# Gating one-hots of a PEER layer interleaved over two tokens instead of four, and the late low splits taken off GpSimd

## The chip, the cores and the metric

The kernel runs on one core of a Trainium2 chip. The metric is device time in microseconds from the start to the end of one execution; the median of three runs is given for the kernel before. The profile is of one more execution.

## The reference, cut to what matters

Two transformer blocks on 256 tokens of 1024 features. The part that matters here is the PEER feed-forward, which runs once in each of the first two layers:

```python
def peer_ffn(h, w_query, sub_keys, expert_u, expert_v):
    ...
    scores = jnp.einsum('thpd,hpkd->thpk', q, sub_keys.astype(jnp.float32))
    s_top, i_top = lax.top_k(scores, K)
    cand = (s_top[:, :, 0, :, None] + s_top[:, :, 1, None, :]).reshape(T, Hh, K * K)
    cand_idx = (i_top[:, :, 0, :, None] * PEER_NKEYS + i_top[:, :, 1, None, :]).reshape(T, Hh, K * K)
    best, pos = lax.top_k(cand, K)
    expert_idx = jnp.take_along_axis(cand_idx, pos, axis=-1)
    gates = jax.nn.softmax(best, axis=-1).astype(h.dtype)
    ...
        u = expert_u[idx]
        a = jax.nn.gelu(jnp.einsum('tkd,td->tk', u, xb)) * g
        return jnp.einsum('tk,tkd->td', a, expert_v[idx])
```

Each token picks 128 of 16384 = 128 x 128 experts (8 heads of 16) and sums their outputs with gates.

## The kernel before, in words

The kernel computes all 16384 experts for all tokens and multiplies by a dense gate matrix that is zero where a token did not pick the expert.

**Units.** Weights come as units of 128 x 1024 float32, 512 KB each. `plan` writes out their order by hand; for a weight unit its last field says whether GpSimd (POOL) or VectorE (DVE) makes the low half. `pump` loads units ahead (four raw buffers, queue SP, L274), then splits each into a high part (ScalarE copy, L286) and a low part (subtraction on DVE or POOL, L288) of type fp32r; three split buffers let it run three units ahead. A product is three matmuls (`mm3`, L321 to L323): high x high, high x low, low x high. In `peer` a layer has 128 units `pu` (scores of 128 experts each) and 128 units `pv` (their outputs).

**Which units go to POOL.** Of a layer's `pu` units, those below 64 with i % 4 = 3 (16 of them) and those from 64 on with i % 3 = 2 (65, 68, ... 125: 21 of them) have their low part made on POOL. All `pv` units have it made on DVE.

**PEER stage by stage.** The first 64 `pu` units fill `S1` (experts 0 to 8191) while routing (top-k) runs on DVE beside them. The second 64 fill `S2`, and beside them runs `gating`: per batch of `GT` = 4 tokens one step, 64 steps a layer, put into the queue of tasks from which `tick` takes about one per unit (four units take one more in their middle). Then come the `pv` units, the products with `V`.

**A gating step** has three parts, each of another batch: `scale(b-2)`, `place(b-1)`, `build(b)`.
- `build` (L1141 to L1150): four DVE operations on 128 x 512 fp16. Two compare `iota_rep` with the indices `i1` and `i2` of four tokens, which gives one-hots `o1` and `og[:, 1]`; two multiply the second one-hot by the high and low part of the gate (`g3`). The layout is [expert key, token], the token innermost: each token's column has a step of four fp16 elements, 8 bytes.
- `place` (L1152 to L1158): for each of the four tokens two matmuls of 128 x 128 fp16, `o1` of the token as the stationary operand and `og` of the token as the moving one, summed in PSUM. Eight matmuls a step, 1024 in the kernel.
- `scale` (L1160 to L1168): DVE multiplies the `S1` slice by the gates from PSUM (L1162), ScalarE copies the other half (L1166), and every fourth step POOL stores it to HBM (L1168) for `gate_late`.

On each engine the order is the order of the program: in one unit DVE has the low split of a unit two ahead, then scale, then the four builds; TensorE has 24 matmuls of the unit, then the eight of `place`. `o1` and `og` have two buffers each.

Of the kernel before, what the change touches and what calls it, by code (L numbers as in the profile page):

```python
# [13 lines left out]
F16 = mybir.dt.float16  # L14
# [3 lines left out]
ALU = mybir.AluOpType  # L18
# [4 lines left out]
P = 128  # L23
# [6 lines left out]
GT = 4  # L30
# [123 lines left out]
class Net:  # L154
# [41 lines left out]
    def plan(self):  # L196
        a = self.a
        self.units = u = []

        def ws(src, tag, every=0):  # L200
            return [("w", src[i], tag, bool(every) and i % every == every - 1) for i in range(src.shape[0])]

        def on_pool(units, *which):
            return [(w[0], w[1], w[2], i in which) for i, w in enumerate(units)]

        def cols(l, lo, hi):
            return [("ada", (l, o)) for o in range(lo, hi)]

        def mix(units, jobs=(), per=1, skip=0):
            jobs = deque(jobs)  # L210
            for i, w in enumerate(units):
                u.append(w)
                for _ in range(per if i >= skip else 0):
                    if jobs:
                        u.append(jobs.popleft())
            u.extend(jobs)

        def spread(units, jobs, every, skip):
            jobs = deque(jobs)
            for i, w in enumerate(units):  # L220
                u.append(w)
                if i >= skip and i % every == 1 and jobs:
                    u.append(jobs.popleft())
            assert not jobs

        mk = ws(a["mem_k"], "mem_k")
        mix(on_pool(ws(a["mem_v"], "mem_v"), 2, 4, 6), cols(0, 0, 16), 2)
        mix(on_pool(ws(a["ret_qk"], "ret_qk"), 0, 1, 3))
        mix(ws(a["ret_g"], "ret_g") + ws(a["ret_v"], "ret_v"), cols(0, 16, 40))
        mix(ws(a["ret_o"], "ret_o"))  # L230
        mix(mk[:3])
        for l in range(2):
            pq = ws(a["pq"][16 * l:16 * l + 16], "pq")
            mix(on_pool(pq, 0, 1, 2, 4, 7, 10, 13))
            us = [("w", a["pu"][P * l + i], "pu", i % 4 == 3 if i < 64 else i % 3 == 2)
                  for i in range(P)]
            vs = [("w", a["pv"][P * l + i], "pv", False) for i in range(P)]
            mix(us)
            if l == 0:
                jobs = cols(0, 40, 48) + cols(1, 0, 37)  # L240
                spread(vs[:64], jobs[:17], 3, 13)
                spread(vs[64:], jobs[17:], 2, 9)
            else:
                mix(vs)
            if l == 0:
                mix(on_pool(mk[3:6], 2))
                mix(on_pool(ws(a["sgu_v"], "sgu_v"), 0, 1, 2) + on_pool(ws(a["sgu_u"], "sgu_u"), *range(0, 24, 4)), cols(1, 37, 48), 1, 6)
                mix(ws(a["sgu_o"], "sgu_o", 4))
                mix(mk[6:8])
        for tag in ("hy_v", "hy_qk", "hy_c", "hy_oc", "hy_oa", "mem_q", "mem_o"):  # L250
            mix(ws(a[tag], tag))
        mix(ws(a["mlp_u"], "mlp_u") + ws(a["mlp_d"], "mlp_d"))
        self.n_load = self.n_split = self.w_done = self.w_split = 0
        self.raw = {}
        self.ring = deque()
        self.flying = [0, 0]
        self.split = deque()
# [270 lines left out]
    def run(self):  # L528
        nc, a = self.nc, self.a
        self.plan()  # L530
        c = self.p_c = self.keep("pc")
        self.p_h = self.keep("ph", bufs=4)
        self.p_raw = self.keep("praw", bufs=RAW_BUFS)
        self.p_split = self.keep("psplit", bufs=SPLIT_BUFS)
        self.p_ps = self.keep("pps", bufs=2, space=PSUM)
        self.p_d = self.keep("pd", space=DRAM)
        self.ident = c.tile([P, P], F32, name="ident")
        self.iota = c.tile([P, TOPK], F32, name="iota")
        self.vecs = c.tile([P, _off], F32, name="vecs")
        self.ones = c.tile([P, P], F32, name="ones")  # L540
        self.eps = c.tile([P, 1], F32, name="eps")
        self.iota_rep = c.tile([P, P, GT], F16, name="iota_rep")
        self.mod = [c.tile([P, 48], F32, name=f"mod{l}") for l in range(2)]
        self.d_c = self.p_d.tile([1, D], F32, name="d_c")
        self.d_mk = self.p_d.tile([P, KC, T], F32, name="d_mk")
        self.d_mv = self.p_d.tile([P, 2, D], F32, name="d_mv")
        self.d_mr = self.p_d.tile([P, T], F32, name="d_mr")
        self.d_g = [self.p_d.tile([T // GS, P, 64, GS], F32, name=f"d_g{l}") for l in range(2)]
        self.d_x = [self.p_d.tile([P, KC, T], F32, name=f"d_x{l}") for l in range(2)]
        self.open_x()  # L550
        cm_f, pf = self.pool("pf0")
        cm_s, ps = self.pool("start", side="right")
        cm_e, self.p_early = self.pool("early", bufs=EARLY_BUFS, side="right")
        mem = ps.tile([P, KC, T], F32, name="mem")
        nc.scalar.dma_start(self.vecs, a["vecs"])
        for k in range(2):
            nc.sync.dma_start(mem[:, 4 * k:4 * k + 4], a["memT"][:, 4 * k:4 * k + 4])
        cr = ps.tile([P, D], F32, name="craw")
        nc.scalar.dma_start(cr, a["c"].to_broadcast([P, D]))
        nc.scalar.dma_start(self.x, a["xT"])  # L560
        nc.vector.memset(self.ones, 1.0 / D)
        nc.vector.memset(self.eps, EPS)
        self.const(self.ident, "ident")
        iota = ps.tile([P, P], F32, name="iota_all")
        self.const(iota, "iota")
        self.cs = pf.tile([P, 2, T], F32, name="cs")
        rope = self.rope(ps, self.cs)

        self.mem_n = 0
        self.mem_pend = deque()  # L570
        mh = self.new_h(pf)
        for n in range(KC):
            self.split_scaled([mh[n]], [mem[:, n]], [self.vec("g_mem", n, 1)])
        self.pump(1)
        self.cact = self.p_n.tile([P, D], F32, tag="cact", name="cact")
        nc.scalar.activation(self.cact, cr, AF.Silu)
        nc.gpsimd.dma_start(self.d_c, self.cact[0:1, :])
        self.ms_begin(KC)
        nc.vector.tensor_copy(self.iota, iota[:, :TOPK])
        nc.vector.tensor_copy(self.iota_rep, iota[:, :, None].to_broadcast([P, P, GT]))  # L580
        def squares(src, n):
            return lambda: [self.ms_add(src[:, n + k]) for k in range(4)]
        st = {}

        def total():
            st[0] = self.ms_root(self.ms_sum(), KC)
            self.ms_begin(KC)

        def rstd():
            self.rstd = self.ms_recip(st[0], "rstd")  # L590
        self.pipe([squares(self.x, 0), lambda: (rope[0](), squares(self.x, 4)()), rope[1],
                   lambda: (rope[2](), total(), squares(mem, 0)()), rstd, squares(mem, 4)])
        self.mem_store_v = self.mem_values(mh)
        self.shut(cm_e)
        self.shut(cm_s)
        self.retention(self.rstd)
        self.fill_pool, self.fill_h = cm_f, mh
        self.peer(0)
        self.sgu()
        self.peer(1)  # L600
        self.hybrid()
        self.memattn()
        self.mlp()
        self.shut(self.cm_deep)
        self.shut(self.cm_x)
# [531 lines left out]
    def gating(self, po, S, i1, i2, g3, d_g):  # L1137
        nc = self.nc
        made, mult, stage = {}, {}, {}

        def build(b):  # L1141
            tt = slice(b * GT, b * GT + GT)
            sh = [P, P, GT]
            o1 = po.tile(sh, F16, tag="o1", name="o1")
            og = po.tile([P, 2, P, GT], F16, tag="og", name="og")
            nc.vector.tensor_tensor(o1, self.iota_rep, i1[:, None, tt].to_broadcast(sh), op=ALU.is_equal)
            nc.vector.tensor_tensor(og[:, 1], self.iota_rep, i2[:, None, tt].to_broadcast(sh), op=ALU.is_equal)
            for k in range(2):
                nc.vector.tensor_tensor(og[:, k], og[:, 1], g3[:, k, None, tt].to_broadcast(sh), op=ALU.mult)  # L1149
            made[b] = (o1, og)  # L1150

        def place(b):  # L1152
            o1, og = made.pop(b)
            g = mult[b] = self.st_tile("g").rearrange("p (t c) -> p t c", t=GT)
            for t in range(GT):
                for k in range(2):
                    nc.tensor.matmul(g[:, t], o1[:, :, t], og[:, k, :, t], start=k == 0, stop=k == 1)  # L1157

        def scale(b):
            g = mult.pop(b).rearrange("p t c -> p c t")  # L1160
# [629 lines left out]
```

## Time and profile before

| | us |
|---|---|
| median of 3 runs | 2640.93 (2640.41 to 2640.95) |
| the profiled execution | 2635.87 |
| its span, first to last instruction | 2634.1 |
| TensorE (PE) busy | 2552.9 (97%) |
| weight loads (PEld) busy | 2488.4 (94%) |
| VectorE (DVE) busy | 1937.0 (74%) |
| ScalarE (ACT) busy | 1262.2 (48%) |
| GpSimd (POOL) busy | 405.5 (15%) |

The share of busy time is an average over stages. Matmuls overlap in their records, so the length of one record is longer than the distance from one to the next; the distance is what a matmul costs in a stream. The chain that ended last is followed back from the last instruction to whatever released each step.

### The profile page before, as it was taken

The page shows a single profiled execution, that of the slowest core. Times are in us where ns is not written, and L with a number is a line of the kernel's source. Part 1 is how long each engine was busy: PE and PEld are TensorE (multiplying, and loading weights), DVE is VectorE, ACT ScalarE, POOL GpSimd, SP SyncE. Part 2 cuts the span into 40 slices and gives each one's busy share as a digit, 9 for nine tenths or more (in the row PEclk, how much of TensorE's full clock was granted, in tenths as well). Part 3 has the DMA queues.
Part 4 walks back from the last instruction along what each step waited for, and adds up shares of the span by engine and source line. Part 5 has one row for each costly group of instructions (what it writes and reads, how often), then busy time and mean ns, then how long its engine had stood idle before and what let it go on. Part 6 is the DMA issues. An engine that isn't in the chain of part 4 may idle for free.

```text
span 2634.1 us, 49904 instructions
## 1 busy us (share of the span) xinstructions
PE 2552.9 (97%) x20358; PEld 2488.4 (94%) x20358; DVE 1937.0 (74%) x3148; ACT 1262.2 (48%) x1790; POOL 405.5 (15%) x252
## 2 busy tenths in 40 slices
PE   5999999999999999999999999999999999989998
PEld 3989999999999999988999999999999999879998
DVE  8777688889868767775777888888675555785754
ACT  4445444444444445455554444444444444665643
POOL 5000312222221000020132222222100000101001
PEclk9999999999999999999999999999999999999999
DMA  7685555554559788867564555555675655444553
GB/s 285 225 301 168 191 176 185 179 174 161 182 177 336 254 299 273 274 229 239 168 208 166 180 181 180 175 166 176 211 278 184 216 185 184 156 136 149 174 189 116
DMA packets 146406, 532.34 MB, mean 202 GB/s; under 512 B 16080, under 2 KB 18256, under 8 KB 145280
## 3 DMA queue, kind: packets, MB, share of 16 engines
q1 hardware_dynamic: 133104, 481.36, 54.9%
q0 software_dynamic: 11584, 45.56, 4.7%
q8 instruction: 160, 2.62, 0.4%
q10 hardware_dynamic: 1488, 2.23, 0.2%
q14 instruction: 70, 0.57, 0.1%
HBM read 506.93 MB, written 22.16 MB: 201 GB/s over the span
## 4 chain that ended last, share of the span: by engine, by line
PE 81%; DVE 9%; DMA 5%; ACT 3%; issue 2%; POOL 0%; DVEq 0%; ACTq 0%; SPq 0%; POOLq 0%
PE pu L322 11%; PE pu L321 11%; PE pu L323 11%; PE V L322 8%; PE V L323 8%; PE V L321 8%; PE g L1157 4%; PE po L322 3%; PE po L323 3%; PE po L321 3%; DVE split L288 2%; ACT split L286 2%; DMA raw<-in_pv 1%; PE pq L322 1%; PE pq L323 1%
## 5 line engine op out<-in xcount | busy, mean ns | idle before, releaser
L288 DVE TENSOR_TENSOR split<-raw,split 128x1024 fp32r<-128x1024 f32 x698 | 856.7, 1231 | 559.9 <-ACT split L286 559.0
L286 ACT ACTIVATE split<-raw 128x1024 fp32r<-128x1024 f32 x808 | 851.4, 1057 | 728.5 <-PE V L323 328.8
L321 PE MATMUL pu<-h,split 128*128 128x256 f32 x2496 | 718.8, 288 | 0.1
L322 PE MATMUL pu<-h,split 128*128 128x256 f32 x2496 | 706.8, 283 | 0.5 <-DVE h L381 0.5
L323 PE MATMUL pu<-h,split 128*128 128x256 f32 x2496 | 705.5, 283 | 1.1 <-POOL split L288 0.9
L323 PE MATMUL V<-a_sp,split 128*128 128x256 f32 x2048 | 579.4, 283 | 2.3 <-DVE split L288 2.3
L322 PE MATMUL V<-a_sp,split 128*128 128x256 f32 x2048 | 579.3, 283 | 0.1
L321 PE MATMUL V<-a_sp,split 128*128 128x256 f32 x2048 | 579.1, 283 | 0.2 <-ACT split L286 0.2
L321 PEld LDWEIGHTS pu<-h,split 128*128 128x128 f32 x2496 | 479.4, 192 | 0.8 <-ACT u L1323 0.3
L322 PEld LDWEIGHTS pu<-h,split 128*128 128x128 f32 x2496 | 477.9, 191 | 1.3 <-DVE h L381 0.7
L323 PEld LDWEIGHTS pu<-h,split 128*128 128x128 f32 x2496 | 477.2, 191 | 1.7 <-POOL split L288 1.3
L288 POOL TENSOR_TENSOR split<-raw,split 128x1024 fp32r<-128x1024 f32 x110 | 276.4, 2513 | 782.9 <-ACT split L286 780.7
L323 PEld LDWEIGHTS V<-a_sp,split 128*128 128x128 f32 x2048 | 392.3, 192 | 3.1 <-DVE split L288 3.1
L322 PEld LDWEIGHTS V<-a_sp,split 128*128 128x128 f32 x2048 | 392.2, 192 | 0.5 <-DVE a_sp L375 0.5
L321 PEld LDWEIGHTS V<-a_sp,split 128*128 128x128 f32 x2048 | 392.3, 192 | 0.4 <-ACT split L286 0.4
L879 ACT ACTIVATE S<-pu 128x512 f32<-128x512 f32 x128 | 76.6, 598 | 273.1 <-PE pu L323 273.1
L1149 DVE TENSOR_TENSOR og<-og,g 128x512 f16<-128x512 f16 x256 | 150.4, 588 | 8.8
L1157 PE MATMUL g<-og,o 128*128 128x128 f16 x1024 | 143.3, 295 | 1.4 <-DVE og L1149 1.4
L408 POOL TENSOR_TENSOR ms_acc<-ms_acc,sq 128x256 f32<-128x256 f32 x45 | 51.4, 1142 | 569.6 <-ACT sq L406 566.1
L293 DVE SCALAR_TENSOR_TENSOR raw<-raw,cact 128x1024 f32<-128x1024 f32 x96 | 126.9, 1329 | 3.2 <-issue 1.6
L1157 PEld LDWEIGHTS <-o 128*128 128x128 f16 x1024 | 103.9, 118 | 9.8 <-issue 2.5
L322 PE MATMUL pq<-h,split 128*128 128x256 f32 x320 | 93.3, 292 | 5.7 <-DVE h L468 4.0
(370 smaller groups left out, 4049.9 us busy)
## 6 DMA issues: line engine op xcount, KB each, us to landing
raw<-in_pu SPq DMA_DIRECT2D x256, 512.0 KB, 3.3
raw<-in_pv SPq DMA_DIRECT2D x256, 512.0 KB, 4.1
raw<-in_ada SPq DMA_DIRECT2D x96, 512.0 KB, 4.7
raw<-in_pq SPq DMA_DIRECT2D x32, 512.0 KB, 4.1
d_g<-stage POOLq DMA_DIRECT2D x32, 512.0 KB, 3.7
g<-d_g POOLq DMA_DIRECT2D x16, 1024.0 KB, 8.6
raw<-in_mlp_u SPq DMA_DIRECT2D x32, 512.0 KB, 3.4
raw<-in_mlp_d SPq DMA_DIRECT2D x32, 512.0 KB, 3.3
```

The costliest lines, as they stand in the source:

```text
L286: nc.scalar.activation(s[:, 0], r, AF.Copy)
L288: eng.tensor_sub(s[:, 1], r, s[:, 0].bitcast(F32))
L293: nc.vector.scalar_tensor_tensor(r, r, 1.0, self.cact, op0=ALU.mult, op1=ALU.mult, accum_out=self.mod[l][:, o:o + 1])
L321: mm(ps, w_hi, x_hi, start=start, stop=False, **kw)
L322: mm(ps, w_hi, x_lo, start=False, stop=False, **kw)
L323: mm(ps, w_lo, x_hi, start=False, stop=stop, **kw)
L408: nc.gpsimd.tensor_add(self.ms_parts[0], self.ms_parts[0], sq)
L879: nc.scalar.activation(S[:, i - 1:i + 1], pt, AF.Gelu_apprx_tanh)
L1149: nc.vector.tensor_tensor(og[:, k], og[:, 1], g3[:, k, None, tt].to_broadcast(sh), op=ALU.mult)
L1157: nc.tensor.matmul(g[:, t], o1[:, :, t], og[:, k, :, t], start=k == 0, stop=k == 1)
```

## The change

Per batch of four tokens the one-hots have the layout [pair of tokens, expert key, token of the pair] instead of [expert key, token]: a token's column has a step of two fp16 elements, 4 bytes, instead of four, 8 bytes. `iota_rep` shrinks from 128 x 4 to 128 x 2 and is read twice by a broadcast. The four DVE operations of `build` keep their 512 elements; their innermost runs have two elements. The eight matmuls of `place` read the same values from the other places. Second, of the `pu` units from 64 on none has its low part made on POOL: these 21 a layer (42 in all) go to DVE.

```diff
-            us = [("w", a["pu"][P * l + i], "pu", i % 4 == 3 if i < 64 else i % 3 == 2)
-                  for i in range(P)]
+            us = [("w", a["pu"][P * l + i], "pu", i < 64 and i % 4 == 3) for i in range(P)]
...
-        self.iota_rep = c.tile([P, P, GT], F16, name="iota_rep")
+        self.iota_rep = c.tile([P, P, 2], F16, name="iota_rep")
...
-        nc.vector.tensor_copy(self.iota_rep, iota[:, :, None].to_broadcast([P, P, GT]))
+        nc.vector.tensor_copy(self.iota_rep, iota[:, :, None].to_broadcast([P, P, 2]))
...
         def build(b):
             tt = slice(b * GT, b * GT + GT)
-            sh = [P, P, GT]
+            sh = [P, GT // 2, P, 2]
+
+            def pairs(v):
+                return v.rearrange("p (a c) -> p a c", c=2)[:, :, None, :].to_broadcast(sh)
+
             o1 = po.tile(sh, F16, tag="o1", name="o1")
-            og = po.tile([P, 2, P, GT], F16, tag="og", name="og")
-            nc.vector.tensor_tensor(o1, self.iota_rep, i1[:, None, tt].to_broadcast(sh), op=ALU.is_equal)
-            nc.vector.tensor_tensor(og[:, 1], self.iota_rep, i2[:, None, tt].to_broadcast(sh), op=ALU.is_equal)
+            og = po.tile([P, 2] + sh[1:], F16, tag="og", name="og")
+            io = self.iota_rep[:, None].to_broadcast(sh)
+            nc.vector.tensor_tensor(o1, io, pairs(i1[:, tt]), op=ALU.is_equal)
+            nc.vector.tensor_tensor(og[:, 1], io, pairs(i2[:, tt]), op=ALU.is_equal)
             for k in range(2):
-                nc.vector.tensor_tensor(og[:, k], og[:, 1], g3[:, k, None, tt].to_broadcast(sh), op=ALU.mult)
+                nc.vector.tensor_tensor(og[:, k], og[:, 1], pairs(g3[:, k, tt]), op=ALU.mult)
             made[b] = (o1, og)
...
-                    nc.tensor.matmul(g[:, t], o1[:, :, t], og[:, k, :, t], start=k == 0, stop=k == 1)
+                    nc.tensor.matmul(g[:, t], o1[:, t // 2, :, t % 2], og[:, k, t // 2, :, t % 2],
+                                     start=k == 0, stop=k == 1)
```

## Rows read from the trace of the kernel before

**Rows 1.** The page: engines' busy time, and the last chain by engine.
```profile
PE 2552.9 (97%) x20358; PEld 2488.4 (94%) x20358; DVE 1937.0 (74%) x3148; ACT 1262.2 (48%) x1790; POOL 405.5 (15%) x252
...
PE 81%; DVE 9%; DMA 5%; ACT 3%; issue 2%; POOL 0%; DVEq 0%; ACTq 0%; SPq 0%; POOLq 0%
```
**Rows 2.** Windows of both gating stretches: length, busy PE, PEld, DVE, ACT, POOL; PEclk, DMA, GB/s.
```profile
530.00:774.00 244.00, 243.32 (x2031) 239.01 (x2030) 209.63 (x361) 102.68 (x160) 56.87 (x36) 1.00 0.51 173
1636.00:1880.00 244.00, 243.25 (x2029) 238.70 (x2027) 209.72 (x362) 102.83 (x161) 56.87 (x36) 1.00 0.52 173
```
**Rows 3.** Timeline of PE around one step: start us, length us, instruction, count.
```profile
547.01 0.28 PE L322 MATMUL pu<-h,split 128*128 128x256 f32 x1
547.13 0.28 PE L323 MATMUL pu<-h,split 128*128 128x256 f32 x1
547.26 1.11 PE L1157 MATMUL g<-og,o 128*128 128x128 f16 x8
...
548.33 0.28 PE L322 MATMUL pu<-h,split 128*128 128x256 f32 x1
```
**Rows 4.** Groups by line and form, PE: busy us, mean ns of one, idle before.
```profile
L322 PE MATMUL pu<-h,split 128*128 128x256 f32 x2496 | 706.8, 283 | 0.5 <-DVE h L381 0.5
...
L1157 PE MATMUL g<-og,o 128*128 128x128 f16 x1024 | 143.3, 295 | 1.4 <-DVE og L1149 1.4
...
L355 PE MATMUL pv<-split,h 128*128 128x512 f32 x176 | 70.5, 401 | 5.2 <-DVE split L288 3.3 <-POOL split L288 1.9
```
**Rows 5.** Timeline of PE in a stream of 512-column matmuls.
```profile
167.83 0.40 PE L355 MATMUL pv<-split,h 128*128 128x512 f32 x1
168.06 0.39 PE L356 MATMUL pv<-split,h 128*128 128x512 f32 x1
```
**Rows 6.** Groups by line and form, weight loads.
```profile
L322 PEld LDWEIGHTS pu<-h,split 128*128 128x128 f32 x2496 | 477.9, 191 | 1.3 <-DVE h L381 0.7
...
L1157 PEld LDWEIGHTS <-o 128*128 128x128 f16 x1024 | 103.9, 118 | 9.8 <-issue 2.5
...
L1487 PEld LDWEIGHTS po<-pT,v 128*64 128x64 f32 x16 | 1.4, 137 | 0.3
```
**Rows 7.** Lines 1146 and 1149 (build): durations ns least/median/most, first and last start.
```profile
L1146 DVE TENSOR_TENSOR o<-iota_rep,i x128: 416/419/2473, 524.9 to 1863.0; 128x512 f16<-128x512 f16 x128
...
L1149 DVE TENSOR_TENSOR og<-og,g x256: 424/425/2517, 525.7 to 1864.3; 128x512 f16<-128x512 f16 x128
```
**Rows 8.** Groups of DVE, 524 to 775 us.
```profile
L1149 DVE TENSOR_TENSOR og<-og,g 128x512 f16<-128x512 f16 x128 | 75.2, 588 | 4.4
L288 DVE TENSOR_TENSOR split<-raw,split 128x1024 fp32r<-128x1024 f32 x45 | 55.1, 1224 | 29.5 <-ACT split L286 29.5
L1146 DVE TENSOR_TENSOR o<-iota_rep,i 128x512 f16<-128x512 f16 x64 | 45.1, 705 | 0.0
```
**Rows 9.** Groups of POOL, 524 to 775 us.
```profile
L288 POOL TENSOR_TENSOR split<-raw,split 128x1024 fp32r<-128x1024 f32 x21 | 50.5, 2407 | 114.5 <-ACT split L286 114.5
```
**Rows 10.** Timeline of POOL and DVE around one POOL split.
```profile
548.66 2.40 POOL L288 TENSOR_TENSOR split<-raw,split 128x1024 fp32r<-128x1024 f32 x1 [3.31 <-ACT split L286]
...
548.87 2.47 DVE L1146 TENSOR_TENSOR o<-iota_rep,i 128x512 f16<-128x512 f16 x1
```
**Rows 11.** Waits of PE, 530 to 774 us (total, times, longest); PE's timeline at one.
```profile
PE g L1157 <- DVE og L1149: 0.7, 4, 0.2
...
539.08 0.28 PE L323 MATMUL pu<-h,split 128*128 128x256 f32 x1
...
539.74 0.98 PE L1157 MATMUL g<-og,o 128*128 128x128 f16 x7 [0.17 <-DVE og L1149]
...
540.67 0.28 PE L322 MATMUL pu<-h,split 128*128 128x256 f32 x1
```
**Rows 12.** Groups by form, DVE: two operations of 512 elements elsewhere.
```profile
L375 DVE TENSOR_TENSOR a_sp<-S,a_sp 128x512 fp32r<-128x512 f32 x128 | 87.5, 685 | 0.9 <-ACT a_sp L374 0.9
...
L1091 DVE TENSOR_TENSOR tree<-tree 128x512 bf16<-128x512 bf16 x8 | 3.4, 427 | 0.3
```

## Prediction

> **What bounds the kernel now.** I read the page's busy times and last chain first: TensorE is busy 97% of the span and makes up 81% of the chain [rows 1]. The average settles nothing for one stage, so next come the windows of the two stretches in which gating runs, 244 us each. There PE is busy 243.3 us of 244 at the full granted clock, 1.00, which is the 2.4 GHz level; DVE is busy 209.6, ACT 102.7, POOL 56.9, DMA half [rows 2]. So these stretches are PE streams without holes, with DVE 34 us behind, and what the eight matmuls of a step cost on PE is paid in full. PE's waits say the same from the other side: 0.7 us in the first stretch, four times, for the builds [rows 11].
>
> Then the timeline of one step. The distance between two `pu` matmuls is 0.12 us. From the last of them before the step to the second one after it pass 548.33 - 547.13 = 1.20 us [rows 3]; less two ordinary distances that is 0.96 us for eight gating matmuls, 0.12 us each. A matmul with 128 columns thus takes as long as a `pu` matmul with 256. Over 1024 of them this is 123 us of the kernel.
>
> **Part one, the step of the operands.** Nothing is added on PE: the same 1024 matmuls and weight loads with a 4-byte step in place of 8. What is a column worth at either step? A 256-column `pu` matmul lasts 283 ns and a 512-column one 401 [rows 4]: 118 ns for 256 columns, 0.46 ns a column, with some 165 ns that do not depend on them. These read 4-byte elements one behind the other, a 4-byte step. The gating matmul lasts 295 ns with 128 columns; less the same 165 that is 130 ns, 1.02 ns a column, a little over twice as much. At 0.46 ns its columns would take 59 and the record would last about 224. The nearest row to the changed access is therefore the `pu` row: other type, same byte step.
>
> Is it the moving operand or the weight load that sets the distance? A load of 128 float32 columns lasts 191 ns and one of 64 lasts 137 [rows 6], so 54 ns for 64 columns and 83 ns of fixed length. The fp16 load lasts 118, which leaves 35 ns for its columns. It runs beside the matmul and is the shorter of the two; I take it as hidden, also at the new step. If it is not, the first rival holds.
>
> In distances: 0.12 us for 256 columns [rows 3] and 0.23 for 512 [rows 5] give 0.43 ns a column and 0.01 us fixed. For 128 columns that is 0.055 + 0.01, and with rounding of the rows I take 0.067 us. Bounds: at best the fixed part vanishes too, 0.055; at worst nothing changes, 0.12. I choose 0.067 because both terms stand in a stream of the same kind, a load and a matmul by turns at a 4-byte step. Saved: (0.12 - 0.067) x 1024 = 54 us, 27 a layer; bounds 0 and 67.
>
> The Trainium skill, page "TensorE: Matmul & The Clock Gate", section "Back-to-back issue gap", gives about 81 ns for a matmul of 128 columns with its weight load in a real kernel. By that figure the saving would be (0.12 - 0.081) x 1024 = 40 us and the time about 2599; no row here shows a 16-bit stream at a smaller step, so this is an estimate from the page.
>
> The builds keep their size. They last 419 to 425 ns in the median [rows 7], where a float32 operation of 512 elements lasts 685 and a bf16 one with runs of four elements 427 [rows 12]: they run at the fast rate of 16-bit data. Runs of two are not in the trace. Bounds: 0 and 685 - 425 = 260 ns each. I take 0, since going down to runs of four costs nothing (427 against 425). The smaller `iota_rep` saves part of one operation at the start, nothing that counts.
>
> **Part two, the low splits.** Per layer 21 POOL splits go, 50.5 us of POOL [rows 9], and 21 of DVE come, at 1.224 us [rows 8]: +25.7 us on DVE. But DVE also loses something. While a POOL split runs from 548.66 to 551.06, the build that started at 548.87 lasts 2.47 us, to 551.34, in place of 0.42 [rows 10]. Such builds show in the sums: the L1149 group has 75.2 us where 128 x 0.425 = 54.4 would do, and L1146 45.1 where 64 x 0.419 = 26.8 would [rows 7, 8]. That is 20.8 + 18.3 = 39.1 us of blocked DVE a layer, which go with the POOL splits. DVE after: 209.6 - 39.1 + 25.7 = 196.2 us a layer, 3.07 a unit, less than before although it does more.
>
> On PE the POOL splits cost little. The four waits are the units with two steps, where a blocked build comes late: 540.67 - 539.08 = 1.59 us in place of 1.20 [rows 3, 11], 0.4 us, four times a layer, 3.2 us in all. A two-step unit still asks two builds of DVE, so I count 2 us of the 3.2.
>
> The order on the queues does not move: no DMA, no wait and no instruction changes its place except the subtraction's engine. POOL keeps its stores of every fourth step, with nothing ahead of them. Behind the added DVE split stand scale and the four builds of the same unit, and PE's `place` wants those one unit later. PE after: 243.3 - 27.1 = 216.2 us a layer, 3.4 a unit against 3.07 on DVE. So PE stays the bound, with 20 us on DVE to spare instead of 34. Loads come sooner by the same share, 173 GB/s becoming some 195 [rows 2], with DMA about half busy; hidden. ACT at 103 us of 216 has room.
>
> **The rivals.**
>
> *The step does not matter to PE.* The gating distance, 0.12, is also that of a stream in which each matmul has one load of 128 columns, and the fp16 load record, 118 ns, is just as long as the distance [rows 3, 6]. If loading 128 columns sets the pace, the step changes nothing. Then only the waits go: 2641 - 3 = 2638. Against it: the 295 ns record, which a 59 ns stream would leave at 224, and the load's own 35 ns. The Trainium skill, page "SBUF — State Buffer", section "Specifications (TRN2)", states that a read has full bandwidth from two hits per 16-byte line; an 8-byte step makes two, so by that rule the change gives nothing. The trace speaks against the rule as far as the 1.02 ns a column do.
>
> *DVE's waits remain.* In the first stretch DVE also stood idle before its splits for 29.5 us and before L1149 for 4.4 [rows 8]. If these do not shrink when PE quickens, DVE needs 196.2 + 34 = 230 us a layer, more than PE's 216, and the saving is 243.3 - 230 = 13 a layer: 2614. For it: the queue is in order, and a split waits for ScalarE. Against it: these waits are there because ScalarE itself follows the PE's pace through three split buffers.
>
> *Slower: the builds lose their fast rate with runs of two.* Place: the four builds of each step. Price: up to 0.26 us each, 256 a layer, 66.6 us. DVE then needs 196.2 + 66.6 = 262.8 us a layer, above the 243.3 of before, and sets the pace: +19.5 a layer, +39, 2680. It decides from 0.08 us a build (DVE level with PE at 216) and makes the kernel slower from (243.3 - 196.2) / 256 = 0.18 us.
>
> **How the numbers follow.** Forecast: 54 + 2 = 56 us off. On the profiled execution 2635.9 - 56 = 2580; that execution stands 5 us under the median of the runs, so against the median 2640.9 - 56 = 2585. Chances: the forecast with its spread 0.78, DVE's waits 0.08, no effect on PE 0.08, builds at the slow rate 0.06. The forecast's own spread is from 2572 (bound 67 + 2 saved) to about 2605. The range reaches to 2612, near DVE's waits, so that the bounds and part of that case lie in it: 2572 to 2612. A measurement of this kernel tells about 0.2%, 5 us, from no change. Faster by more: 0.78 + 0.08 = 0.86; within: 0.08; slower: 0.06.
>
> **What would show it.** Right: L1157 matmuls of about 225 ns, eight of them in some 0.55 us; the second 64 `pu` units of a layer in about 217 us instead of 244, both layers alike; no POOL split there; builds with a longest near the median of 425; DVE about 196 us in that stretch; all other stages as before. Step one is wrong if L1157 stays near 295; the DVE part is wrong if builds stand near 685, or if PE's waits for them grow from 0.7 us to tens.

## The result and the profile after

| | us |
|---|---|
| median of 4 runs of the changed kernel | 2592.9 (2591.8 to 2594.9) |
| median of the kernel before, beside it | 2640.7 (2637.9 to 2641.0) |
| ratio | 0.982, 95% interval 0.981 to 0.984 |
| the profiled execution of the changed kernel | 2594.9 |
| its span | 2593.1 |

The kernel became 48 us faster; 56 were forecast (2585), and the time lies in the range. Line numbers of the changed kernel differ: L1161 is the gating matmul (L1157 before), L1153 and L1150 the builds (L1149, L1146), L1167 scale, L287 the low split, L285 ScalarE's high part.

The two gating stretches of the changed kernel, each from just before its first gating matmul to the start of the products with `V`; they answer to [rows 2] (columns as there):

```profile
532.00:752.00 220.00, 216.27 (x2028) 212.40 (x2028) 192.12 (x381) 100.74 (x160) 8.52 (x16) 1.00 0.56 189
1618.00:1838.00 220.00, 216.27 (x2028) 212.40 (x2028) 192.20 (x381) 100.82 (x160) 8.54 (x16) 1.00 0.56 189
```

Each has become 24 us shorter, 244 to 220; the two together are the 48 us by which the medians differ. The spans of the two profiled executions differ by 41 only: outside the stretches the later one took 7 us more, 4 of them in the products with `V` of the first layer (377 us against 373). Another profiled execution of the changed kernel, `r_changed` below, has 373 there too, so this is scatter between executions and not an effect of the change. DVE's work fell from 209.6 to 192.1 although it took over 21 splits (196.2 was forecast), and the work of PE fell to 216.3 (216.2 was forecast). But PE is no longer busy all the time: 216.3 of 220.

One ordinary step on PE's timeline (answers to [rows 3]), then the groups of the gating matmul and its weight load (answer to [rows 4, 6]):

```profile
547.92 0.28 PE L322 MATMUL pu<-h,split 128*128 128x256 f32 x1
548.05 0.63 PE L1161 MATMUL g<-og,o 128*128 128x128 f16 x8
548.49 0.36 PE L320 MATMUL pu<-h,split 128*128 128x256 f32 x1
548.69 0.28 PE L321 MATMUL pu<-h,split 128*128 128x256 f32 x1
```
```profile
L1161 PE MATMUL g<-og,o 128*128 128x128 f16 x1024 | 82.5, 220 | 7.5 <-DVE og L1153 7.5
```
```profile
L1161 PEld LDWEIGHTS <-o 128*128 128x128 f16 x1024 | 59.2, 97 | 15.2 <-DVE og L1153 7.3 <-issue 2.8
```

A step now takes 548.69 - 547.92 = 0.77 us in place of 1.20: 0.43 us less, 55 us over 128 steps. The eight last 0.63 us from the first start to the last end, so less the 0.22 of one record they stand (0.63 - 0.22) / 7 = 0.058 us apart; before it was (1.11 - 0.295) / 7 = 0.116 [rows 3, 4]. Eight times the difference is 0.46 us, a little more than the 0.43 of the step. The rest went at the seam behind the eight. The first `pu` matmul there has a long record and the next one starts late in both kernels; this is the row of the kernel before, which stands between those of [rows 3]:

```profile
548.12 0.37 PE L321 MATMUL pu<-h,split 128*128 128x256 f32 x1
```

From the start of the last gating matmul (the first start and seven distances) to the second `pu` matmul pass 548.69 - 548.46 = 0.23 us now and 548.33 - 548.07 = 0.26 before. One gating and one `pu` distance would be 0.18 and 0.24, so the seam costs about 0.05 us where it cost 0.02. A likely reason is that the weight load of a `pu` unit, 0.19 us [rows 6], has only one short gating matmul to hide behind; no run tests this.

Builds and splits on DVE, answering to [rows 7, 8] (the first fence is the line's durations, the second the groups from 526 to 753 us):

```profile
L1153 DVE TENSOR_TENSOR og<-og,g x256: 424/425/430, 530.1 to 1824.1; 128x512 f16<-128x512 f16 x128
```
```profile
L287 DVE TENSOR_TENSOR split<-raw,split 128x1024 fp32r<-128x1024 f32 x66 | 80.6, 1221 | 26.4 <-ACT split L285 26.4
L1153 DVE TENSOR_TENSOR og<-og,g 128x512 f16<-128x512 f16 x128 | 54.4, 425 | 4.4
L1150 DVE TENSOR_TENSOR o<-iota_rep,i 128x512 f16<-128x512 f16 x64 | 26.7, 417 | 0.0
```

The builds kept 425 ns with runs of two elements, and the long ones of 2.5 us are gone: the longest lasts 430.

What went the other way is PE's wait for builds (answers to [rows 11]):

```profile
PE g L1161 <- DVE og L1153: 3.7, 8, 0.7
...
539.87 0.28 PE L322 MATMUL pu<-h,split 128*128 128x256 f32 x1
540.86 0.23 PE L1161 MATMUL g<-og,o 128*128 128x128 f16 x1 [0.71 <-DVE og L1153]
541.32 0.57 PE L1161 MATMUL g<-og,o 128*128 128x128 f16 x7 [0.23 <-DVE og L1153]
541.69 0.36 PE L320 MATMUL pu<-h,split 128*128 128x256 f32 x1
541.89 0.28 PE L321 MATMUL pu<-h,split 128*128 128x256 f32 x1
```

This is the end of the first two-step unit. From 539.87 to 541.89 pass 2.02 us in place of 0.77: 1.25 us lost, at each of the eight such units, 10 us in the kernel, where before it was 0.4 each, 3 in all. So 55 - 7 = 48 us. DVE and ScalarE at this place show why; first DVE, then ScalarE:

```profile
536.55 0.89 DVE L1153 TENSOR_TENSOR og<-og,g 128x512 f16<-128x512 f16 x2
538.12 1.23 DVE L287 TENSOR_TENSOR split<-raw,split 128x1024 fp32r<-128x1024 f32 x1 [0.68 <-ACT split L285]
539.26 0.41 DVE L1167 TENSOR_TENSOR S<-S,g 128x256 f32<-128x256 f32 x1
...
541.18 0.41 DVE L1167 TENSOR_TENSOR S<-S,g 128x256 f32<-128x256 f32 x1
```
```profile
536.27 0.60 ACT L878 ACTIVATE S<-pu 128x512 f32<-128x512 f32 x1 [2.34 <-PE pu L322]
536.76 0.38 ACT L1171 ACTIVATE stage<-g 128x256 f32<-128x256 f32 x1
537.02 1.06 ACT L285 ACTIVATE split<-raw 128x1024 fp32r<-128x1024 f32 x1
```

(L878 is the gelu, L1171 the copy in `scale`.) In a two-step unit DVE has a split and then scale and builds twice. The matmuls at the end of the unit want the builds made in its middle. These stand behind the split, which stands behind ScalarE's high part, which here stands behind a gelu; DVE sits idle for 0.68 us, begins scale and builds at 539.26 and ends them at about 541.2, while PE was ready at about 540.0.

### The profile page after: what moved, and what is told of

Read it like the earlier page. It is cut to its first block, busy times and chain, and to the rows that moved or that the text cites. A ratio compares the mean times of both kernels' runs of the same rounds, so it can differ in the third digit from the quotient of the medians.

```text
span 2593.1 us, 49906 instructions
## 1 busy us (share of the span) xinstructions
PE 2505.1 (97%) x20358; PEld 2441.9 (94%) x20358; DVE 1905.0 (73%) x3190; ACT 1258.9 (49%) x1790; POOL 303.2 (12%) x210
## 4 chain that ended last, share of the span: by engine, by line
PE 81%; DVE 9%; DMA 4%; ACT 4%; issue 2%; POOL 1%; DVEq 0%; ACTq 0%; SPq 0%; POOLq 0%
PE pu L320 11%; PE pu L321 11%; PE pu L322 11%; PE V L321 9%; PE V L322 9%; PE V L320 9%; PE po L321 3%; PE po L322 3%; PE po L320 3%; DVE split L287 3%; PE g L1161 2%; ACT split L285 2%; PE pq L321 1%; PE pq L322 1%; PE pq L320 1%
## 5 line engine op out<-in xcount | busy, mean ns | idle before, releaser
L287 DVE TENSOR_TENSOR split<-raw,split 128x1024 fp32r<-128x1024 f32 x740 | 907.9, 1230 | 558.8 <-ACT split L285 558.1
L285 ACT ACTIVATE split<-raw 128x1024 fp32r<-128x1024 f32 x808 | 850.8, 1057 | 711.1 <-PE V L322 334.8
L287 POOL TENSOR_TENSOR split<-raw,split 128x1024 fp32r<-128x1024 f32 x68 | 175.3, 2579 | 553.7 <-ACT split L285 551.5
L878 ACT ACTIVATE S<-pu 128x512 f32<-128x512 f32 x128 | 76.5, 597 | 234.8 <-PE pu L322 234.8
L1153 DVE TENSOR_TENSOR og<-og,g 128x512 f16<-128x512 f16 x256 | 108.8, 425 | 8.8
L1171 ACT ACTIVATE stage<-g 128x256 f32<-128x256 f32 x128 | 48.8, 382 | 109.6 <-DVE S L1167 109.6
L320 PE MATMUL pq<-h,split 128*128 128x256 f32 x320 | 95.9, 300 | 3.5 <-ACT h L465 1.9
L321 PE MATMUL pq<-h,split 128*128 128x256 f32 x320 | 93.6, 292 | 4.7 <-DVE h L467 3.2
```

Of the source, the lines that this page charges most:

```text
L285: nc.scalar.activation(s[:, 0], r, AF.Copy)
L287: eng.tensor_sub(s[:, 1], r, s[:, 0].bitcast(F32))
L320: mm(ps, w_hi, x_hi, start=start, stop=False, **kw)
L321: mm(ps, w_hi, x_lo, start=False, stop=False, **kw)
L878: nc.scalar.activation(S[:, i - 1:i + 1], pt, AF.Gelu_apprx_tanh)
L1153: nc.vector.tensor_tensor(og[:, k], og[:, 1], pairs(g3[:, k, tt]), op=ALU.mult)
```

## The experiments

**The two parts, each alone.** The layout without the splits' move:

```diff
-            us = [("w", a["pu"][P * l + i], "pu", i < 64 and i % 4 == 3) for i in range(P)]
+            us = [("w", a["pu"][P * l + i], "pu", i % 4 == 3 if i < 64 else i % 3 == 2)
+                  for i in range(P)]
```

> The changed kernel, but the late low splits stay on GpSimd as before (21 a layer). Theory: the layout alone gives the faster matmuls, 0.057 us from one to the next in place of 0.118, and the splits on DVE matter because a GpSimd split holds a build up for some 2.1 us. At the faster pace that comes on top of the waits at the two-step units, which grow from 1.25 us each to 2 or 2.5: 8 to 12 us over the changed kernel, some 2603 us. Rival: where the splits are made is worth nothing, since DVE has room either way: the time of the changed kernel, 2593 within 3.

Measured: 2596.1 us (2594.6 to 2596.6); ratio to before 0.984 (0.982 to 0.985). PE's waits for builds in the whole kernel, then the builds' durations:

```profile
PE g L1162 <- DVE og L1154: 9.8, 16, 1.2
```
```profile
L1154 DVE TENSOR_TENSOR og<-og,g x256: 424/425/2511, 526.4 to 1826.6; 128x512 f16<-128x512 f16 x128
```

The layout carries nearly all of the gain. Builds of 2.5 us are back, but PE's waits grow only from 7.5 us in the changed kernel to 9.8, not by 8 to 12; the expected 2603 was too much. Because runs on different chips stood some us apart, both were timed once more side by side:

> The changed kernel as it is, on the same chip as the two below, since the runs so far stood on several chips and differ by a few us there: 2593 within 3 by every theory.

> The changed kernel with the late low splits on GpSimd, once more beside the changed kernel. Theory from the first run (waits at the two-step units 12.3 us in all against 10.1): 2 us over the changed kernel. Rival: no difference within 1 us.

Measured: 2590.3 us (2587.7 to 2592.7) for the changed kernel, 2592.5 (2591.4 to 2594.8) with the layout alone, and in the profiles the same waits for builds as in the first pair, 7.5 and 9.8 us. The medians lie apart by what the waits do, 2 us; the runs overlap, so the times alone would not show it.

The splits' move without the layout is the reverse edit, made to the kernel before:

> The kernel before with only the late low splits moved to DVE; the layout of four tokens stays. Theory: matmuls stay at 0.118 us from one to the next, TensorE stays the bound, and only the eight waits of 0.4 us at the two-step units change: 2638 to 2641 us, builds at 425 ns without the long ones. Rival: the freed DVE carries a part of the gain of the whole change: clearly under 2635.

Measured: 2639.2 us; ratio to before 0.9997 (0.9988 to 1.0007). The builds' durations, the first stretch, and PE at the first two-step unit:

```profile
L1148 DVE TENSOR_TENSOR og<-og,g x256: 424/425/429, 528.5 to 1864.9; 128x512 f16<-128x512 f16 x128
```
```profile
530.00:774.00 244.00, 243.32 (x2032) 239.18 (x2032) 194.28 (x381) 103.77 (x160) 8.53 (x16) 1.00 0.51 171
```
```profile
539.65 0.29 PE L1156 MATMUL g<-og,o 128*128 128x128 f16 x1
540.10 0.98 PE L1156 MATMUL g<-og,o 128*128 128x128 f16 x7 [0.17 <-DVE og L1148]
```

DVE loses its 15 us of work (209.6 to 194.3), and PE's 243.32 do not move. Even the waits at the two-step units stay, 0.17 us as before [rows 11]: the builds held up by POOL were not what made them.

**Which operand's step it is.** In the changed kernel the stationary one-hots go back to the layout of four tokens, the moving ones stay; and the other way round:

```diff
-            o1 = po.tile(sh, F16, tag="o1", name="o1")
+            s4 = [P, P, GT]
+            o1 = po.tile(s4, F16, tag="o1", name="o1")
...
-                    nc.tensor.matmul(g[:, t], o1[:, t // 2, :, t % 2], og[:, k, t // 2, :, t % 2],
+                    nc.tensor.matmul(g[:, t], o1[:, :, t], og[:, k, t // 2, :, t % 2],
```

> The changed kernel with the moving one-hots (og) at a step of 4 bytes and the stationary ones (o1) back at 8 bytes. Theory (the moving operand's step sets the distance, the weight load is hidden): 0.057 to 0.06 us from matmul to matmul, matmul records of 218 ns, 2593 us within 5. Rival (the weight load sets the distance): 0.118 us, 2593 + 55 = 2648 less the waits that go, some 2638.

> The other half: the stationary one-hots (o1) at 4 bytes, the moving ones (og) at 8. Theory: 0.118 us from matmul to matmul, records of some 297 ns, 2638 us. Rival (the weight load sets it): 0.057 us and 2593. If both operands count, a distance between the two here and in the kernel with the other half.

Measured: 2594.8 us (ratio 0.983, 0.981 to 0.985) with only the moving operand at 4 bytes, 2636.7 (ratio 0.9992, 0.9982 to 1.0001) with only the stationary one. Matmul and weight load, first where only the moving operand is at 4 bytes, then where only the stationary one is:

```profile
L1162 PE MATMUL g<-og,o 128*128 128x128 f16 x1024 | 86.4, 225 | 6.9 <-DVE og L1154 6.9
```
```profile
L1162 PEld LDWEIGHTS <-o 128*128 128x128 f16 x1024 | 65.2, 115 | 14.5 <-DVE og L1154 6.8 <-issue 2.5
```
```profile
L1162 PE MATMUL g<-og,o 128*128 128x128 f16 x1024 | 141.4, 294 | 1.4 <-DVE og L1154 1.4
```

The moving operand's step carries the gain. The weight load of 115 ns at 8 bytes hides nearly all of itself beside the matmuls; it is not wholly without a price, since busy PE in the group rises from 82.5 to 86.4 us, 4 us in the kernel. The rival that the load sets the pace falls.

**How the cost goes with the step.** A larger one: the layout of four tokens with a gap of four elements behind each key, for the moving operand only (the stationary one at 8 bytes):

```diff
-            og = po.tile([P, 2] + sh[1:], F16, tag="og", name="og")
+            og = po.tile([P, 2, P, 2 * GT], F16, tag="og", name="og")[:, :, :, 0:GT]
```

> The changed kernel with the moving one-hots at a step of 16 bytes (the layout of four tokens with a gap of four elements after each key) and the stationary ones at 8. Theory (cost in proportion to the bytes stepped over, from 4 bytes on): four cycles a column, a record of 165 + 213 = 378 ns, 0.21 to 0.23 us from matmul to matmul, 2640 + 1024 x 0.1 = some 2740 us. Rival (any step over 4 bytes costs the same): records of 297 ns, 0.118 us, some 2638.

Measured: 2748.6 us, in a single run. A smaller one, 2 bytes, each token's keys side by side:

```diff
-            sh = [P, GT // 2, P, 2]
+            sh = [P, GT, P]
...
-                return v.rearrange("p (a c) -> p a c", c=2)[:, :, None, :].to_broadcast(sh)
+                return v[:, :, None].to_broadcast(sh)
...
-                    nc.tensor.matmul(g[:, t], o1[:, t // 2, :, t % 2], og[:, k, t // 2, :, t % 2],
+                    nc.tensor.matmul(g[:, t], o1[:, t], og[:, k, t],
```

> The changed kernel with each token's 128 keys side by side, a step of 2 bytes; the index is then one element read 128 times along the innermost run of the builds. Theory: at 4 bytes a column already goes at one cycle, so matmul records stay at 218 ns and the distance at 0.057 us; if instead bytes alone set the pace, the record falls to about 190. For the builds this is the slower rival's case: if they fall to about 685 ns, DVE needs 192 + 66.6 = 259 us a layer, sets the pace, and the kernel takes 2593 + 2 x (259 - 220) = 2671 us; if they keep 425 ns it takes 2593.

Measured: 2683.2 us, also in a single run. The matmul groups, first at 16 bytes, then at 2; below them eight matmuls on the timeline, first at 16 bytes, then at 2:

```profile
L1161 PE MATMUL g<-og,o 128*128 128x128 f16 x1024 | 257.4, 408 | 0.0
```
```profile
L1161 PE MATMUL g<-og,o 128*128 128x128 f16 x1024 | 97.3, 221 | 68.3 <-DVE og L1153 68.1
```
```profile
550.34 2.02 PE L1161 MATMUL g<-og,o 128*128 128x128 f16 x8
```
```profile
549.94 0.62 PE L1161 MATMUL g<-og,o 128*128 128x128 f16 x8
```

At 16 bytes the distance is (2.02 - 0.41) / 7 = 0.23 us, at 2 it is (0.62 - 0.22) / 7 = 0.057. The records by step are 221, 220, 295 and 408 ns at 2, 4, 8 and 16 bytes; the distances 0.058, 0.12 and 0.23 at 4, 8 and 16 double with the step. (The record at 16 bytes was expected at 378, some 30 less.) At 2 bytes nothing more is to be had. Only fp16 was tried at several steps, so the runs do not tell a rule in bytes from one in elements. The kernel at 2 bytes is slower all the same, because of the builds, whose group this is, with the first stretch behind it:

```profile
L1153 DVE TENSOR_TENSOR og<-og,g 128x512 f16<-128x512 f16 x256 | 177.1, 692 | 8.8
```
```profile
530.00:785.00 255.00, 220.90 (x1933) 206.91 (x1931) 250.67 (x374) 97.39 (x151) 8.00 (x15) 0.97 0.45 153
```

With the index or the gate read as one element along the innermost run, the builds slow down to 692 ns (this group; the two comparisons take 685), and DVE is busy 250.7 us of 255 while PE waits for it. This is the slower rival of the prediction as it looks when it comes true: 2683 against the 2680 worked out for it. The 2671 expected for this run was 12 too low.

**The waits at the two-step units.** The extra step moved from even to odd units:

```diff
-        u_units(S2, 70, early, (2, 14, 26, 38))
+        u_units(S2, 70, early, (3, 15, 27, 39))
```

> The changed kernel with its four extra steps a layer in the middle of units 3, 15, 27, 39 instead of 2, 14, 26, 38. Theory of the 1.25 us that TensorE waits at each of them: DVE's split stands ahead of the builds and waits for ScalarE's high part, which in an even unit stands behind a gelu of 0.6 us; in an odd unit it doesn't, so each wait falls to some 0.65 us and the kernel by 5 us, 2588. Rival (DVE simply has two steps of work in one unit): waits and time stay, 2593.

Measured: 2588.3 us (2584.3 to 2592.3); ratio to before 0.981 (0.980 to 0.982). DVE and PE at the first two-step unit:

```profile
538.96 1.22 DVE L287 TENSOR_TENSOR split<-raw,split 128x1024 fp32r<-128x1024 f32 x1
540.10 0.41 DVE L1167 TENSOR_TENSOR S<-S,g 128x256 f32<-128x256 f32 x1
```
```profile
541.04 0.28 PE L322 MATMUL pu<-h,split 128*128 128x256 f32 x1
541.69 0.23 PE L1161 MATMUL g<-og,o 128*128 128x128 f16 x1 [0.37 <-DVE og L1153]
...
542.72 0.28 PE L321 MATMUL pu<-h,split 128*128 128x256 f32 x1
```

DVE no longer idles before its split, and the place costs 542.72 - 541.04 = 1.68 us, 0.91 over an ordinary step instead of 1.25. The gelu ahead of ScalarE's high part was a good quarter of the wait; the rest stays although nothing holds DVE up there. It is put down to the two steps' work itself, and the next run gives that work more room. A loss of 0.65 was expected and 0.91 came, so this theory was half right. The median falls about as expected, but the runs spread over 8 us, more than the 2.7 us that the waits explain.

Builds two steps ahead of their matmuls, with a third buffer:

```diff
-            o1 = po.tile(sh, F16, tag="o1", name="o1")
+            o1 = po.tile(sh, F16, tag="o1", name="o1", bufs=3)
...
-            if 0 <= b - 2 < n:
-                scale(b - 2)
-            if 0 <= b - 1 < n:
-                place(b - 1)
+            if 0 <= b - 3 < n:
+                scale(b - 3)
+            if 0 <= b - 2 < n:
+                place(b - 2)
```

> The changed kernel with builds two steps ahead of their matmuls instead of one (three buffers of the one-hots in place of two, scale three behind). Theory: the waits at the two-step units, 10 us in all, are builds that come one unit too late; they go, and the kernel takes 2583. Rival: DVE's total work catches up elsewhere, or the longer way to the store costs at the end of the stretch: 2593 or more.

Measured: 2585.2 us (2582.3 to 2586.7); ratio to before 0.980 (0.978 to 0.981). The first stretch:

```profile
532.00:752.00 220.00, 219.94 (x2064) 216.80 (x2063) 194.19 (x381) 104.76 (x165) 8.55 (x16) 1.00 0.57 194
```

PE is busy 219.94 of 220 us again and waits for no build (the stretch itself is now over some 7 us ahead of the window's end). So the wait was that of builds made one unit too late. Last, the same with the late splits back on POOL:

> Builds two steps ahead and the late low splits on GpSimd. Theory: a GpSimd split harms only by making a build late, and with a step more of room no build is late, so TensorE's waits for builds are under 1 us and the time is that of builds two ahead with the splits on DVE, 2585 within 2. Rival: DVE loses so much to GpSimd that it falls behind (209.6 us of work in a stretch of 216 and waits on top): 2590 or more.

Measured: 2585.1 us (2581.6 to 2585.3); ratio to before 0.980 (0.978 to 0.981). The first stretch, and a build's group in it:

```profile
532.00:752.00 220.00, 219.90 (x2066) 216.88 (x2066) 205.99 (x361) 106.21 (x165) 56.86 (x36) 1.00 0.58 194
```
```profile
L1151 DVE TENSOR_TENSOR o<-iota_rep,i 128x512 f16<-128x512 f16 x62 | 62.2, 1003 | 0.0
```

The one build next to the splits lasts 1003 ns in the mean, and PE does not notice. With a step of room the place of the splits is worth nothing. The last one beats the changed kernel on the same chip (2590.3) by 5 us; the one ahead of it, on another chip, stands 54 us under the kernel before there, where the changed kernel stands 48 under.

## Why the prediction was right, and where not

- *PE bounds the gating stretches, and a step's matmuls are paid in full.* Right: 0.43 us less a step on PE came out as 24 us less a stretch (64 x 0.43 = 27.5, less 3.5 of new waits), and DVE alone relieved of 15 us moved nothing.
- *The moving operand's byte step sets the distance; the load is hidden.* Right for the distance, and shown by the two halves (2594.8 and 2636.7); the load at 8 bytes is hidden but for some 4 us. The choice between float32 and fp16 rows went by the byte step, and the record came to 220 ns where 224 was worked out.
- *0.067 us a matmul, 54 us.* Measured as the prediction did it, the step less two ordinary distances, it is (0.77 - 0.24) / 8 = 0.066, and the step's saving is 0.43 us: 55 us. That it fits so well is partly luck. Inside the eight the distance is 0.058, less than forecast, and the seam behind them, which was not in the sum, takes the difference.
- *Builds cost nothing more.* Right: 425 ns. The price of the other case was right as well, as the kernel at 2 bytes shows.
- *DVE does less although it does more.* Right in size (196 forecast, 192 measured). In worth the 2 us of the forecast came out by luck: alone the move changes nothing clear of noise, and beside the layout it saves 2 us of waits that come only with the faster pace.
- *The two-step units give 2 us back.* This is the term that failed: they cost 7 us more. The prediction ascribed their 0.4 us to builds held up by POOL; with those gone the wait stayed at 0.17 us. It is work that stands in one queue: split, scale, four builds, scale, four builds in one unit. PE got through the unit some 0.9 us sooner, and the whole of that appeared as waiting. The mean of 3.07 us of DVE against 3.4 of PE hid it, since in these units DVE has 5 us. That is the rival "DVE's waits remain" on four units a layer; on the others it did not come, although DVE's idle time before its splits fell only from 29.5 to 26.4 us. That time was slack: with builds two ahead and the splits on POOL, DVE works 206 us in the same window, and PE waits for no build.
- With 55 - 7 = 48 us the account closes.

The Trainium skill, page "SBUF — State Buffer", section "Specifications (TRN2)", would have an 8-byte step at full bandwidth, with two hits in each 16-byte line; its row adds, without a figure, that each cross to a new line has a price. For TensorE's moving operand the trace disagrees with the first: 0.12 us at 8 bytes against 0.058 at 4. That 16 bytes, with one hit a line, are slower, 0.23, the page has too.

The Trainium skill, page "TensorE: Matmul & The Clock Gate", section "Back-to-back issue gap", gives 81 ns for 128 columns with their load; here eight in a row stand 58 ns apart, and the 40 us worked out from 81 were too few.

## What to carry to other kernels

In these runs a strided fp16 moving operand costs TensorE in proportion to its step from 4 bytes to 16, the widest tried, so the order of an operand in SBUF is a term of the matmul's price; interleave just as far as the engine that builds it needs for its fast rate. When a stage's bound is made faster, look at its busiest unit and not at its mean: a queue that kept up on average came late exactly where one unit held two steps. A buffer more, so that the maker runs two steps ahead, gave the rest back here, and made the choice of engine for the splits indifferent.

## What the runs showed of the hardware

- A matmul of 128 fp16 columns lasts 221, 220, 295 and 408 ns with the moving operand at steps of 2, 4, 8 and 16 bytes (granted clock in the stretch 0.97 at 2 bytes, 1.00 at the others): level up to 4, then 14 to 16 ns more a byte in the distance ((0.12 - 0.058) / 4 and (0.23 - 0.12) / 8).
- The weight load of 128 fp16 columns lasts 97 ns at 4 bytes and 115 to 118 at 8, far less of a difference, and stays hidden but for 4 us over the 1024 of them (matmuls busy 86.4 us against 82.5).
- An fp16 operation of 512 elements on DVE keeps 425 ns with innermost runs of two elements, and takes 692 when one input is a single element repeated along the run.
